# Both blocks' 32-row gate matmuls issued back to back, each in its own rows and its own bank

## The chip, the cores and the metric

The kernel runs on one core of a Trainium2 chip. The metric is the device time of one execution in microseconds (us); the time of before is the median of three runs. Five engines work side by side: PE (TensorE, matmuls), DVE (VectorE), ACT (ScalarE), POOL (GpSimd) and SP (SyncE, which here only issues DMAs). Each takes its instructions strictly in the order in which the program lists them; semaphores make one wait for another.

## The reference, cut to what matters

The program is one layer of a hybrid decoder: a gated linear attention (GLA) and a short convolution side by side, an output projection, a SwiGLU feed-forward network and norms, on 2048 positions of width 1024, in float32. The part that the change touches is the forget gate:

```python
gate_logits = (p_a @ w_gate_up[l] + b_gate[l]).astype(jnp.float32)   # p_a: rank 16, 256 gate columns
log_a = (jax.nn.log_sigmoid(gate_logits) / GATE_NORMALIZER).reshape(bsz, seq, GLA_HEADS, GLA_DK)
o = gla_chunked(q, k, v, log_a)      # cumulative sums of log_a within a chunk, exp of them on q and k
```

"The forget gate's second product" is `p_a @ w_gate_up`. Its contraction is short: 16 true rows, kept here as a high and a low part, so 32 rows.

## The kernel before, in words

Positions are cut into four blocks of 512, and two blocks make a half. The kernel goes through half 0 and half 1 in turn: the input projection `in_proj` (L596) runs twelve weight units of width 256, each by a fast matrix product of seven smaller products (`unit`, L370). A matmul of those is L366, L367 or L368 (`product_step`): the float32 operands are split into a high and a low part, so every weight quarter `wq` is made by one ACT copy (L153, high) and one DVE subtraction (L154, low), and L368 is the first matmul that needs the low part. Results are combined in `copied` (ACT, L386) and `plus` (DVE, L390).

Everything else of this stage is background work. Each is a Python generator; `tick` (L201), called after every one of the seven products, advances the first generator of the list `background` to its next `yield`. For half 0 the list holds the row statistics, `gate(0)`, then `h1_ahead` (normalised operands of half 1, made ahead); for half 1 it holds `gate(1)`, and behind it `gla_half(1)`, which `in_proj` appends when half of its units are out. The generators only give the program's order; a list scheduler then moves instructions within each engine by its own estimates, keeping every dependence.

`gate` (L547) makes one product `a` for both blocks of the half; its rows 0 to 31 belong to block j = 0, rows 32 to 63 to j = 1. Then for each block j and each half i of the 256 gate columns it issues one float32 matmul `z` (L571) of 32 rows, 128 columns and 512 positions, into a PSUM bank of its own, and calls `forget_gate` (L577). That is a chain: ACT L580 (abs) and DVE L581 read `z`; ACT L582, L583 (exp, log); DVE L584; four DVE scans L587; ACT L590 (`em`); DVE L591 (the differences `t2`); ACT L592 (`el`); DVE L593 (`dn`); and the store of `t2` to DRAM, `s_d[b][i]` (L594). After each of the four calls the generator yields.

`gla_load` (L675) reads for a chunk of 128 positions of block b, over the SP queue, q and k (`kq`), both stores `s_d[b][0]` and `s_d[b][1]` (`ee`), v (`vt`) and the output gate (`gt`). ACT L681 and L682 take exponentials of `ee`, DVE L683 and L684 multiply them into `kq`, and the PE matmuls L694 (`sc`, 64 rows each, alternating between two row groups and two banks) need both. So the first GLA chunk of a half needs both column halves i = 0 and i = 1 of that half's first block.

POOL forms sums of weight quarters (L349 to L356) and, in `h1_ahead`, differences of operands (L254 to L267).

Of the kernel before, what the change touches and what calls it, by code (L numbers as in the profile page):

```python
# [18 lines left out]
P = 128  # L19
# [32 lines left out]
def tile_hymba_block(ctx, tc, x, xt, win, wa, wgu, wout, wffn, wdown, wdown_first, small, out):  # L52
# [36 lines left out]
    wgu_sb = mixer.tile([64, 256], F32, name="wgu_sb")  # L89
# [42 lines left out]
    def col(c):  # L132
        return sml[:, c : c + 1]

    def bank(name="mm"):
        return ps.tile([P, PB], F32, name=name, tag="mm")
# [4 lines left out]
    def bt(name, shape=(P, PB)):  # L141
        return bx[0].tile(list(shape), F32, name=name, tag="b")
# [4 lines left out]
    def store(dst, src):  # L147
        return nc.sync.dma_start(dst, src)
# [398 lines left out]
    def gate(half, ops):  # L547

        a = bank("a_ps")
        names = "B11", "T1", "B21", "B22"
        for n in names:
            for k in range(4):
                q = {"B11": 3 * k + 1, "T1": 3 * k, "B21": 2 * k + 13, "B22": 2 * k + 12}[n]
                w = wa_sb[:, 32 * q : 32 * q + P]
                for e in range(2):
                    pe.matmul(
                        a[:], w, ops[n][k][:, e, :], start=(n, k, e) == ("B11", 0, 0),
                        stop=n == "B22" and k == 3 and e == 1, skip_group_check=True,  # L560
                    )
        a_sb = bt("a_sb")
        act.activation(a_sb[:], a[:], AF.Copy)
        yield
        for j in range(2):
            small = decays[2 * half + j] = [
                mtiny.tile([P, 2, PT], F32, name=n, tag=n, bufs=4) for n in ("em", "dn", "el")
            ]
            for i in range(2):
                z, r = bank("z"), slice(32 * j, 32 * j + 32)  # L570
                pe.matmul(  # L571
                    z[:], wgu_sb[r, i * P : (i + 1) * P], a_sb[r, :], start=True, stop=True
                )
                forget_gate(2 * half + j, i, z, *small)
                yield

    def forget_gate(b, i, z, em, dn, el):  # L577
        bg = col(C_BG + i)
        t1, t2 = bt("g1"), bt("g2")
        act.activation(t1[:], z[:], AF.Abs, bias=bg)  # L580
        dve.tensor_scalar(t2[:], z[:], bg, 0.0, ALU.add, ALU.min)  # L581
        act.activation(t1[:], t1[:], AF.Exp, scale=-1.0)  # L582
        act.activation(t1[:], t1[:], AF.Ln, bias=one_t)  # L583
        dve.tensor_tensor(t2[:], t2[:], t1[:], ALU.subtract)  # L584
        for t in range(PT):
            s = slice(t * P, (t + 1) * P)
            dve.tensor_tensor_scan(t1[:, s], ones[:], t2[:, s], 0.0, ALU.mult, ALU.add)  # L587
        bs = t1.rearrange("p (a b) -> p a b", b=P)
        dd = t2.rearrange("p (a b) -> p a b", b=P)
        act.activation(em[:, i, :], bs[:, :, 63], AF.Exp, scale=1.0 / 16.0)  # L590
        dve.tensor_tensor(dd, bs, bs[:, :, 63:64].to_broadcast([P, PT, P]), ALU.subtract)  # L591
        act.activation(el[:, i, :], dd[:, :, P - 1], AF.Exp, scale=1.0 / 16.0)  # L592
        dve.tensor_tensor(dn[:, i, :], em[:, i, :], el[:, i, :], ALU.mult)  # L593
        store(s_d[b][i][:], t2[:])  # L594
# [77 lines left out]
    decays = {}  # L672
# [378 lines left out]
    for i in range(4):  # L1051
# [3 lines left out]
    background.extend(  # L1055
        [
            gate_weights(), pause(9), row_stats(2), row_stats(3), gate(0, ops), unhurried(),
            h1_ahead(),
        ]
    )  # L1060
    in_proj(0, ops, first, differences)
    drain_background(lambda: len(background) < 2)
    ops = load_pairs(s_h1)
    background.append(gate(1, ops))
    in_proj(1, ops)
    drain_background(lambda: (1, PT - 1) in done)
# [119 lines left out]
```

## Time and profile before

| what | value |
|---|---|
| median of three runs | 2113.87 us (2112.77 to 2115.74) |
| the profiled execution: span from first to last instruction | 2109.1 us |
| PE busy | 2033.1 us, 96% of the span |
| DVE, ACT, POOL busy | 67%, 48%, 46% |
| `z` matmuls (L571) | 16 records for 8 calls, between 124.8 and 483.4 us |
| mean granted TensorE clock | 0.992 |

The span is the time between the first and the last instruction of one profiled execution; the time of a run also holds what lies around it, 4.8 us between this span and the median. [...] Matmul records overlap: what a matmul costs its successors is read from the distance between starts, not from its duration.

### The profile page before, as it was taken

What the parts mean: (1) busy time and instruction counts of PE and PEld (TensorE: products, weight loads), DVE (VectorE), ACT (ScalarE), POOL (GpSimd) and SP (SyncE); (2) the same over time, 40 slices, a digit from 0 to 9 for tenths busy, and PEclk for the clock granted to TensorE, in tenths of its full rate; (3) what the DMA queues carried; (4) which work ended last, traced back from release to release, by engine and by line L of the source; (5) the groups of instructions that cost most, each with busy time, mean ns of one, the idle gap of its engine ahead of it and who ended that gap; (6) DMA issues with size and microseconds to landing.
All of it is one profiled execution on the core that took longest, in us unless ns stands there. A gap on an engine that the chain in (4) does not pass through costs nothing.

```text
span 2109.1 us, 26874 instructions
## 1 busy us (share of the span) xinstructions
PE 2033.1 (96%) x9133; PEld 1648.9 (78%) x9133; DVE 1418.4 (67%) x1983; ACT 1014.1 (48%) x1997; POOL 972.4 (46%) x703
## 2 busy tenths in 40 slices
PE   5999999999999999999999999999999989999996
PEld 4778888877888878788888878787888868877775
DVE  7669786549753786788786665554766666665564
ACT  5555455656542356445545443333554554543344
POOL 3436322222102464564464348764645544436774
PEclk9999999999999999999999999999999999999998
DMA  7349485425586872656545687697454535587763
GB/s 277 126 158 318 139 329 164 148 83 164 201 284 235 325 249 100 241 198 221 217 172 220 243 327 272 235 338 296 158 207 179 206 134 190 183 344 281 269 269 110
DMA packets 189241, 464.43 MB, mean 220 GB/s; under 512 B 19824, under 2 KB 65072, under 8 KB 179504
## 3 DMA queue, kind: packets, MB, share of 16 engines
q1 hardware_dynamic: 189104, 462.72, 60.4%
q8 instruction: 72, 1.18, 0.2%
q14 instruction: 65, 0.53, 0.1%
HBM read 297.49 MB, written 165.15 MB: 219 GB/s over the span
## 4 chain that ended last, share of the span: by engine, by line
PE 70%; DVE 8%; DMA 7%; ACT 3%; issue 3%; POOL 2%; SPq 0%; DVEq 0%; ACTq 0%; POOLq 0%
PE mm L366 21%; PE mm L368 21%; PE mm L367 21%; DVE wq L154 2%; DMA op<-shT 1%; DVE so L154 1%; PE mm L794 1%; DVE h L490 1%; PE mm L795 1%; PE mm L797 1%; DVE op L154 1%; DMA sx<-y 1%; ACT wq L153 1%; PE o_ps L718 1%; DMA shT<-so 1%
## 5 line engine op out<-in xcount | busy, mean ns | idle before, releaser
L366 PE MATMUL mm<-op,wq 128*128 128x512 f32 x2499 | 981.3, 395 | 23.8 <-DVE c L390 7.8
L368 PE MATMUL mm<-op,wq 128*128 128x512 f32 x2499 | 966.1, 392 | 12.6 <-DVE wq L154 11.9
L367 PE MATMUL mm<-op,wq 128*128 128x512 f32 x2499 | 976.0, 391 | 0.0
L154 DVE TENSOR_TENSOR wq<-raw,wq 128x512 fp32r<-128x512 f32 (+2 forms) x626 | 527.3, 849 | 329.9 <-ACT wq L153 324.3
L153 ACT ACTIVATE wq<-raw 128x512 fp32r<-128x512 f32 (+2 forms) x626 | 363.6, 587 | 555.8 <-PE mm L368 402.4
L366 PEld LDWEIGHTS mm<-op,wq 128*128 128x128 f32 x2499 | 470.8, 188 | 137.6 <-ACT wq L153 12.3
L368 PEld LDWEIGHTS mm<-op,wq 128*128 128x128 f32 x2499 | 470.5, 188 | 123.5 <-DVE wq L154 24.8
L367 PEld LDWEIGHTS mm<-op,wq 128*128 128x128 f32 x2499 | 471.2, 189 | 96.7 <-issue 1.0
L351 POOL TENSOR_TENSOR raw<-s,raw 128x512 f32<-128x512 f32 (+2 forms) x97 | 127.5, 1314 | 422.2 <-DVE wq L154 402.0
L390 DVE TENSOR_TENSOR c<-mm,c 128x512 f32<-128x512 f32 x267 | 183.0, 686 | 95.7 <-PE mm L368 93.0
L349 POOL TENSOR_TENSOR s<-raw 128x512 f32<-128x512 f32 (+2 forms) x97 | 130.2, 1343 | 216.2 <-DMA raw<-in_wffn_dram 88.8
L356 POOL TENSOR_TENSOR raw<-raw 128x512 f32<-128x512 f32 (+2 forms) x97 | 126.7, 1306 | 135.3 <-DVE wq L154 128.1
L386 ACT ACTIVATE c<-mm 128x512 f32<-128x512 f32 x267 | 154.7, 585 | 38.0 <-PE mm L368 36.8
L776 POOL TENSOR_TENSOR ssx<-ssx,q 128x512 f32<-128x512 f32 x52 | 76.5, 1483 | 156.0 <-ACT q L775 155.8
L350 POOL TENSOR_TENSOR raw<-raw 128x512 f32<-128x512 f32 (+2 forms) x97 | 135.1, 1393 | 4.1
L965 POOL TENSOR_TENSOR y<-c,y 128x512 f32<-128x512 f32 x66 | 98.7, 1499 | 49.0 <-DVE c L390 46.6
L154 DVE TENSOR_TENSOR so<-t,so 128x512 fp32r<-128x512 f32 x100 | 91.2, 918 | 25.9 <-ACT so L153 25.4
L153 ACT ACTIVATE wq<-s 128x512 fp32r<-128x512 f32 (+2 forms) x97 | 56.9, 586 | 93.5 <-PE mm L368 83.3
L794 PE MATMUL mm<-op,wq 128*128 128x512 f32 x256 | 100.9, 395 | 0.0
L795 PE MATMUL mm<-op,wq 128*128 128x512 f32 x256 | 99.8, 390 | 0.0
L154 DVE TENSOR_TENSOR wq<-s,wq 128x512 fp32r<-128x512 f32 (+2 forms) x97 | 84.1, 867 | 15.6 <-ACT wq L153 15.0
L153 ACT ACTIVATE so<-t 128x512 fp32r<-128x512 f32 x100 | 62.5, 627 | 41.8 <-DMA sa_T<-so 16.1
(177 smaller groups left out, 1885.0 us busy)
## 6 DMA issues: line engine op xcount, KB each, us to landing
raw<-in_wffn_dram SPq DMA_DIRECT2D x44, 1024.0 KB, 5.7
sa_T<-so SPq DMA_DIRECT2D x88, 512.0 KB, 5.3
op<-sa_T SPq DMA_DIRECT2D x88, 512.0 KB, 9.2
sa_B<-so SPq DMA_DIRECT2D x69, 512.0 KB, 3.4
op<-sa_B SPq DMA_DIRECT2D x69, 512.0 KB, 9.0
raw<-in_win_dram SPq DMA_DIRECT2D x23, 1024.0 KB, 5.5
raw<-in_wdown_dram SPq DMA_DIRECT2D x24, 768.0 KB, 6.2
sx<-y SPq DMA_DIRECT2D x48, 256.0 KB, 3.2
```

The costliest lines, as they stand in the source:

```text
L153: last_hi[:] = [act.activation(hi, src, AF.Copy)]
L154: return dve.tensor_tensor(lo, src, hi.bitcast(F32), ALU.subtract)
L349: pool.tensor_tensor(s1, a21, a22, ALU.add)
L350: pool.tensor_tensor(a21, a11, a21, ALU.subtract)
L351: pool.tensor_tensor(a11, s1, a11, ALU.subtract)
L356: pool.tensor_tensor(a12, a12, a11, ALU.subtract)
L366: pe.matmul(o[:], wh, xh, start=first and k == 0, stop=False, skip_group_check=True)
L367: pe.matmul(o[:], wh, xl, start=False, stop=False, skip_group_check=True)
L368: return pe.matmul(o[:], wl, xh, start=False, stop=k == n - 1, skip_group_check=True)
L386: act.activation(t[:], o[:], AF.Copy)
L390: dve.tensor_tensor(t[:], o[:], t[:], ALU.add)
L794: pe.matmul(o[e, j][:], wh, m[:, 0, :], start=k == 0, stop=False)
```

## The change

The loops over column halves i and blocks j change places. Both blocks' tiles `em`, `dn`, `el` are made first; then for each i both matmuls are issued with nothing between them, into two banks, and the two calls of `forget_gate` follow, with one yield after each as before. The number of matmuls, banks, calls, yields and stores is the same. The order of the four calls was (j, i) = (0,0), (0,1), (1,0), (1,1); it becomes (0,0), (1,0), (0,1), (1,1).

```diff
         for j in range(2):
-            small = decays[2 * half + j] = [
+            decays[2 * half + j] = [
                 mtiny.tile([P, 2, PT], F32, name=n, tag=n, bufs=4) for n in ("em", "dn", "el")
             ]
-            for i in range(2):
-                z, r = bank("z"), slice(32 * j, 32 * j + 32)
+        for i in range(2):
+            z = [bank("z") for _ in range(2)]
+            for j in range(2):
+                r = slice(32 * j, 32 * j + 32)
                 pe.matmul(
-                    z[:], wgu_sb[r, i * P : (i + 1) * P], a_sb[r, :], start=True, stop=True
+                    z[j][:], wgu_sb[r, i * P : (i + 1) * P], a_sb[r, :], start=True, stop=True
                 )
-                forget_gate(2 * half + j, i, z, *small)
+            for j in range(2):
+                forget_gate(2 * half + j, i, z[j], *decays[2 * half + j])
                 yield
```

Lines below the change stand three higher in the changed kernel: `forget_gate` is L580, its differences `t2` L594, and `sc` L697.

## The prediction

> **What bounds the kernel now.** I read the page first, then the PE timeline around the `z` matmuls, then the stretches beside them, then DVE, POOL and ACT in the one stretch where something is late. What I say of the changed order is read from the list of instructions that the scheduler gives each engine in the built program.
>
> ```profile
> span 2109.1 us, 26874 instructions
> PE 2033.1 (96%) x9133; PEld 1648.9 (78%) x9133; DVE 1418.4 (67%) x1983; ACT 1014.1 (48%) x1997; POOL 972.4 (46%) x703
> PE 70%; DVE 8%; DMA 7%; ACT 3%; issue 3%; POOL 2%; SPq 0%; DVEq 0%; ACTq 0%; POOLq 0%
> ```
>
> PE is busy 96% of the span and is 70% of the chain that ended last. So a microsecond taken from PE is worth a microsecond, unless PE then waits at the next place where it is only just served. The tile view gives the removable work, the stretches say where PE has company.
>
> ```profile
> L571 PE MATMUL z<-a_sb,wgu_sb x16: 587/588/692, 124.8 to 483.4; 32*128 32x512 f32 x16
> 160.00:220.00 60.00, 59.40 (x260) 48.65 (x261) 56.90 (x66) 31.61 (x62) 38.26 (x25) 1.00 0.88 297
> 470.00:520.00 50.00, 50.00 (x239) 38.40 (x239) 47.64 (x90) 32.79 (x80) 10.86 (x8) 1.00 0.44 142
> 520.00:600.00 80.00, 80.00 (x439) 65.72 (x438) 56.91 (x109) 42.37 (x116) 9.98 (x7) 1.00 0.66 223
> ```
>
> In each stretch the busy times stand as PE, PEld, DVE, ACT, POOL. Just behind the gates of either half DVE is busy nearly all the time as well: 56.90 of 60 us, and 47.64 of 50. There PE and DVE run neck and neck, and that decides this case.
>
> **The PE time that goes.** A call alone, and two calls in series on the same rows:
>
> ```profile
> 124.44 0.39 PE L368 MATMUL mm<-op,wq 128*128 128x512 f32 x1
> 124.76 1.12 PE L571 MATMUL z<-a_sb,wgu_sb 32*128 32x512 f32 x2
> 125.81 0.50 PE L366 MATMUL mm<-op,wq 128*128 128x512 f32 x1
> 126.15 0.40 PE L367 MATMUL mm<-op,wq 128*128 128x512 f32 x1
> 126.38 0.39 PE L368 MATMUL mm<-op,wq 128*128 128x512 f32 x1
> ...
> 132.43 0.39 PE L368 MATMUL mm<-op,wq 128*128 128x512 f32 x1
> 132.75 1.98 PE L571 MATMUL z<-a_sb,wgu_sb 32*128 32x512 f32 x4
> 134.66 0.50 PE L366 MATMUL mm<-op,wq 128*128 128x512 f32 x1
> ```
>
> The normal step between two starts is 0.23 (126.15 to 126.38). Alone: 125.81 - 124.44 = 1.37, less 0.23, plus the longer step behind it (0.34 for 0.23), is 1.25. Two in series: 134.66 - 132.43 = 2.23, less 0.23, plus 0.11, is 2.11. Before has three groups in half 0 (1, 1 and 2 calls) and four single ones in half 1: 2 x 1.25 + 2.11 = 4.61 and 4 x 1.25 = 5.00. The changed order has two pairs in each half, at the places of the first and of the third call. A pair in different rows and banks costs at least one call, 1.25, and at most two in series, 2.11. Which it is near, the 64-row `sc` matmuls show, which alternate between two row groups and two banks:
>
> ```profile
> 495.10 0.37 PE L694 MATMUL sc<-kq 64*128 64x128 f32 x1
> 495.10 0.38 PE L694 MATMUL sc<-kq 64*128 64x128 f32 x2
> ```
>
> One record takes 0.37, two of different rows 0.38: they run together. I take 1.26 a pair. PE then saves 4.61 - 2.52 = 2.09 in half 0 and 5.00 - 2.52 = 2.48 in half 1, 4.57 in all; at 2.11 a pair it would be 0.39 and 0.78.
>
> [...] The 0.37 and 0.38 above speak for the larger saving, though with 128 columns; what follows needs neither.
>
> **Half 0: what is late next.** Behind the gates PE already waits, and for DVE:
>
> ```profile
> 151.46 0.50 PE L368 MATMUL mm<-op,wq 128*128 128x512 f32 x1 [2.11 <-DVE wq L154]
> 160.60 0.50 PE L366 MATMUL mm<-op,wq 128*128 128x512 f32 x1 [0.86 <-ACT c L386]
> ...
> 150.73 0.68 DVE L154 TENSOR_TENSOR wq<-s,wq 128x512 fp32r<-128x512 f32 x1
> 151.33 0.74 DVE L490 SCALAR_TENSOR_TENSOR h<-h,sml,rb_ps 128x512 f32<-128x512 f32 x1
> 151.99 1.40 DVE L154 TENSOR_TENSOR lo<-t,hi 128x512 fp32r<-128x512 f32 x1
> ```
>
> PE stood 2.11 us until DVE had split the `s` quarter. Coming 2.09 earlier only makes that wait longer, as far as DVE ends at the same time. The scheduler now lists the `h` and the `lo<-t` of this fence ahead of that split, not behind it, so the split ends up to 0.66 (151.99 - 151.33) + 1.40 = 2.1 later, while the splits after it have that work already behind them. The wait of 0.86 can disappear. DVE has the same instructions in all, and through 220 us it is at 56.90 of 60. Half 0 is therefore worth between -0.9 and +2.1; I take 0, DVE's sum being unchanged.
>
> **Half 1: the step that costs.** `gla_load` of block 2 needs both column halves of block 2. Their calls were the first and the second; now they are the first and the third, the second belonging to block 3. So the store `s_d[2][1]`, the `ee` load behind it, ACT's two exponentials, DVE's two products into `kq` and the `sc` matmuls hang on the third gate call instead of the second. PE keeps `sc` at its old place, ahead of the fourth product, and waits there in order. This is how DVE stood in before, from the scans of the third call on:
>
> ```profile
> 487.27 3.39 DVE L587 TENSOR_TENSOR_SCAN g<-ones,g 128x128 f32<-128x128 f32 x4
> 490.58 0.66 DVE L390 TENSOR_TENSOR c<-mm,c 128x512 f32<-128x512 f32 x1
> 491.16 0.74 DVE L635 SCALAR_TENSOR_TENSOR c<-u,sml,c 128x512 f32<-128x512 f32 x1
> 491.82 0.68 DVE L584 TENSOR_TENSOR g<-g,g 128x512 f32<-128x512 f32 x1
> 492.43 0.68 DVE L154 TENSOR_TENSOR wq<-raw,wq 128x512 fp32r<-128x512 f32 x1
> 493.03 0.68 DVE L591 TENSOR_TENSOR g<-g 128x512 f32<-128x512 f32 x1
> 493.63 0.42 DVE L683 TENSOR_TENSOR kq<-kq,ee 128x256 f32<-128x256 f32 x1
> 493.96 0.74 DVE L635 SCALAR_TENSOR_TENSOR c<-u,sml,c 128x512 f32<-128x512 f32 x1
> 494.63 0.42 DVE L684 SCALAR_TENSOR_TENSOR kq<-kq,ee 128x256 f32<-128x256 f32 x1
> 494.96 1.37 DVE L587 TENSOR_TENSOR_SCAN g<-ones,g 128x128 f32<-128x128 f32 x4
> ```
>
> `kq` was ready at 494.63 + 0.42 = 495.05 and `sc` began at 495.10, PE not having waited: already then there was no slack. The third call's L591 ended at 493.71. In the changed list the same instructions stand ahead of it but for one L635 (0.66 to the next start) and one split L154 (0.60). PE also reaches the third call 1.25 earlier, of which I take half, 0.6, because ACT now has two gate chains in a row (bounds 0 and 1.25). It ends at 493.71 - 1.26 - 0.6 = 491.85. Behind it:
>
> ```profile
> 493.74 0.32 SPq L148 DMA_DIRECT2D sd<-g  x1
> sd<-g SPq DMA_DIRECT2D x4, 256.0 KB, 2.1
> DMA to landing us min/median/max: 1.9/2.9/5.0
> 490.81 0.40 ACT L681 ACTIVATE ee<-ee 128x256 f32<-128x256 f32 x1
> 491.25 0.42 ACT L682 ACTIVATE ee<-ee 128x256 f32<-128x256 f32 x1
> ```
>
> The store issues 0.03 after L591 (493.74 - 493.71), lands after 2.1, the `ee` load (the third row is the tile view of `ee`, 466 to 520 us) after 2.9; the exponentials take 491.67 - 490.81 = 0.86, the last product 0.42, `sc` follows 0.05 later. 491.85 + 0.03 + 2.1 + 2.9 + 0.86 + 0.42 + 0.05 = 498.2, against 495.10 before: **+3.1**. PE would be there at 495.10 - 2.48 = 492.6, so it waits about 5.6 and its whole saving is inside that wait. Lower end: the four scans took 3.39 beside POOL's sums and 1.37 without them, 2.02 less; were that not to recur and both landings 1.9, `kq` would be there at 495.0: -0.1. Upper end: none of the 0.6, both landings 5.0: +8.7.
>
> ```profile
> 487.09 1.29 POOL L349 TENSOR_TENSOR s<-raw 128x512 f32<-128x512 f32 x1 [4.02 <-DMA raw<-in_win_dram]
> 488.46 1.29 POOL L350 TENSOR_TENSOR raw<-raw 128x512 f32<-128x512 f32 x1
> ```
>
> [...]
>
> Queued behind `sc` on PE are the transposes and the rest of the unit; the next split that PE needs, the fourth quarter's, is listed ahead of `kq` on DVE, so it is ready. From 520 to 600 PE is busy 80.00 of 80: a delay at 498 is carried to the end. What DVE has queued behind `kq` (the next `u`, then the fifth quarter's split, which PE needs later) is delayed with it, and PE is delayed as much.
>
> **Sum.** 0 for half 0 and +3.1 for half 1 on a span of 2109.1 give 2112.2; the median lies 4.8 above that span, so 2113.87 + 3.1 = **2117.0**. (0.2%, about what a measurement of this kernel can tell from no change, is 4.2 us.)
>
> **Rivals.** *The saving survives, faster.* If `kq` is not late, PE keeps 4.57: 2109.3. For it: PE is 70% of the chain. Against: the 2.11 of waiting in half 0, and 495.05 for 495.10 in half 1. Chance 0.07; half 1 alone surviving, 2111.4, another 0.10.
>
> *The wait at `sc` is dearer, clearly slower.* Two DMAs in series now stand in PE's path, on an SP queue that issues other loads between them. With landings of 5.0 each this gives +8.7, 2122.6. It counts as slower once store and load together take over 6.1 (5.0 taken, plus 4.2 - 3.1), or, together with the +2.1 of half 0, once over 4.0. Chance 0.38.
>
> *The matmuls do not overlap*: 2.11 a pair. PE then comes to `sc` at 494.3, still before 498.2, and the time is again 2117.0; contained in the others.
>
> My forecast, a wait at `sc` that costs a little more than was saved, has 0.45. With the 0.10 it makes 0.55 for within 0.2%, 0.07 faster, 0.38 slower. The range leaves out the first rival and the far end of the second: 2112.5 to 2122.
>
> **What would show it.** Right: each pair of `z` takes about 1.1 us on PE for four records; `sc` in half 1 starts near 498 with an idle time of several us ahead of it, ended by DVE `kq` (L686 or L687), DVE idle before that for ACT `ee` or the load; PE's wait near 150 us lasts 3 to 6. Wrong: no wait ahead of `sc`, or an L594 of the third call well before 490, or new waits for `wq` behind 500.

## Result, and the profile after

The changed kernel took **2122.86 us** (median of 10 runs, 2116.57 to 2126.72) beside 2113.31 us for the kernel before (10 runs, 2104.47 to 2118.0): ratio 1.0047, 95% interval 1.0033 to 1.0061, so 7 to 13 us slower. Measured again beside three of the experiments it was 2119.81 against 2113.22: 1.0033, 1.0019 to 1.0046. The forecast was 2117.0.

From the page of the changed kernel: span, the first row of part 1, and the chain of part 4.

```profile
span 2125.0 us, 26875 instructions
PE 2038.8 (96%) x9133; PEld 1654.2 (78%) x9133; DVE 1412.5 (66%) x1983; ACT 1013.9 (48%) x1997; POOL 973.8 (46%) x703
PE 74%; DVE 10%; DMA 6%; issue 3%; ACT 3%; POOL 2%; SPq 0%; DVEq 0%; ACTq 0%; POOLq 0%
```

PE's busy sum did not fall, although its two pairs in each half are faster: 2038.8 for 2033.1. A busy sum counts longer matmuls too (below, 10 fill 3.40 us at a granted clock of 0.51, where 17 fill 3.50 at 1.00); the mean granted clock is 0.987 for 0.992. The shares alone say no more, so the two traces have to be laid side by side.

**Where the time went.** PE runs 2499 matmuls of L366 in every kernel of this study. I take the start of the n-th one in each trace, counted from 0, and subtract that of before. Between the 75th (110 us in before) and the 250th (244 us) stand half 0's gates and what follows on them; between the 450th (410 us) and the 600th (546 us) those of half 1. A growing difference is time lost there.

| kernel | half 0 | half 1 | between the halves | time, ratio to before (95%) |
|---|---|---|---|---|
| changed | +6.63 | +3.83 | +0.02 | 1.0047 (1.0033 to 1.0061) |
| changed, again (e5) | +4.47 | +4.79 | +0.01 | 1.0033 (1.0019 to 1.0046) |
| e1, half 0 alone | +4.58 | -0.23 | +0.02 | 1.0009 (1.0000 to 1.0017) |
| e2, half 1 alone | +0.01 | +3.42 | 0.00 | 1.0014 (1.0005 to 1.0022) |
| e10, half 1 alone, again | -0.01 | +3.45 | +0.01 | 1.0015 (1.0004 to 1.0025) |
| e3, order without pairs | -0.21 | +4.43 | +0.02 | 1.0017 (1.0007 to 1.0028) |
| e4, pairs of one block | +4.30 | -0.27 | -0.01 | 1.0025 (1.0016 to 1.0034) |
| e6, half 0, one ACT wait mended | +2.52 | -0.22 | 0.00 | 0.9999 (0.9986 to 1.0012) |
| e7, half 0, both mended | +0.43 | -0.18 | +0.02 | 0.9999 (0.9988 to 1.0011) |
| e8, half 1: four in front | +1.11 | -1.63 | +0.03 | 0.9984 (0.9971 to 0.9996) |
| e11, the same again | +0.99 | -1.62 | +0.01 | 0.9988 (0.9978 to 0.9997) |
| e12, e7 and e8 together | +0.43 | -1.60 | +0.01 | 0.9990 (0.9978 to 1.0002) |
| e9, e2 with the wait filled | +0.08 | +1.87 | +0.03 | 0.9998 (0.9988 to 1.0008) |

The rest of a trace wanders without regard to the change: ahead of the 75th matmul the kernels stand -2.9 to +1.2, and between the 1200th and the 1350th they lose either about 0 or about 1.5; the changed kernel did both, 1.51 in its first trace and -0.12 in the second. Behind the 1350th it lost 3.41 and -0.05, and e8 and e11, which are one kernel, 5.38 and 1.51. So of the 15.9 by which the two profiled spans differ (2125.0 to 2109.1) only 10.5 are the change's, which the medians, 9.6 apart, agree with. The two profiled executions are also not alike: in every run that has both numbers on record the time is 1.7 to 2.1 above the span, so of the 4.8 between span and median of before the larger part is an execution quicker than the median, while that of the changed kernel (2126.72) was the longest of its ten.

How far a stretch wanders that nobody changed can be read from the table as well: in e2, e8, e9, e10 and e11 half 0 is that of before, instruction by instruction on every engine, and it stands between -0.01 and +1.11.

**Half 0.** The pairs do what they should. PE, timeline:

```profile
125.64 0.39 PE L368 MATMUL mm<-op,wq 128*128 128x512 f32 x1
125.96 1.13 PE L573 MATMUL z<-a_sb,wgu_sb 32*128 32x512 f32 x4
127.02 0.50 PE L366 MATMUL mm<-op,wq 128*128 128x512 f32 x1
```

Two calls of two records each, and 127.02 - 125.64 - 0.23 + 0.11 = 1.26 for both. By the 100th L366 PE is 2.13 ahead of where it was. Then it waits, for longer than before did in the same place. PE, timeline:

```profile
143.17 0.50 PE L366 MATMUL mm<-op,wq 128*128 128x512 f32 x1 [0.98 <-ACT c L386]
147.84 0.50 PE L366 MATMUL mm<-op,wq 128*128 128x512 f32 x1 [1.20 <-ACT wq L153]
149.47 0.50 PE L368 MATMUL mm<-op,wq 128*128 128x512 f32 x1 [0.90 <-DVE wq L154]
153.19 0.50 PE L368 MATMUL mm<-op,wq 128*128 128x512 f32 x1 [1.13 <-DVE wq L154]
```

These four are 4.21 together, where before had one of 2.11: the saving of 2.1 went into them, as forecast (two of the four are waits for ACT, which the forecast did not name). What was not forecast comes 50 and 70 us later, where before had no wait at all. All engines, timeline:

```profile
199.42 1.30 POOL L254 TENSOR_TENSOR t<-h 128x512 f32<-128x512 f32 x1
...
200.76 0.63 ACT L153 ACTIVATE hi<-t 128x512 fp32r<-128x512 f32 x1 [4.72 <-POOL t L254]
...
202.29 1.08 ACT L386 ACTIVATE c<-mm 128x512 f32<-128x512 f32 x2
...
202.93 0.50 PE L366 MATMUL mm<-op,wq 128*128 128x512 f32 x1 [2.19 <-ACT c L386]
...
220.02 0.90 SPq L145 DMA_DIRECT2D ee<-sd  x2
222.50 0.42 ACT L684 ACTIVATE ee<-ee 128x256 f32<-128x256 f32 x1 [5.32 <-DMA ee<-sd]
...
223.79 0.58 ACT L386 ACTIVATE c<-mm 128x512 f32<-128x512 f32 x1
...
224.42 0.50 PE L366 MATMUL mm<-op,wq 128*128 128x512 f32 x1 [2.15 <-ACT c L386]
```

ACT, 48% busy over the span, stood still for 4.72 and for 5.32 us in front of an instruction that could not start: once `hi<-t`, which needs POOL's `t`; once the exponential of the second chunk, whose `ee` load SP had only just issued. Behind it stood the copies `c<-mm` that take PE's sums out of PSUM, ready to run, and PE waited for the free bank. In the kernel before, ACT had the same instructions the other way round:

```profile
197.30 1.08 ACT L386 ACTIVATE c<-mm 128x512 f32<-128x512 f32 x2
198.76 0.63 ACT L153 ACTIVATE hi<-t 128x512 fp32r<-128x512 f32 x1 [0.38 <-POOL t L254]
...
217.55 1.07 ACT L386 ACTIVATE c<-mm 128x512 f32<-128x512 f32 x2
...
219.95 0.42 ACT L681 ACTIVATE ee<-ee 128x256 f32<-128x256 f32 x1 [0.54 <-DMA ee<-sd]
```

There the copies ran first, and the waits of `hi<-t` and of the exponential hurt nobody. The scheduler had turned both pairs round, 70 and 90 us behind the gates' last products (132.68).

**Half 1.** The forecast wait is there. All engines, timeline (with the three added lines, L594 is the L591 of before, L684 to L687 are L681 to L684, L697 is L694):

```profile
492.10 1.36 DVE L590 TENSOR_TENSOR_SCAN g<-ones,g 128x128 f32<-128x128 f32 x4
...
494.18 2.23 POOL L349 TENSOR_TENSOR s<-raw 128x512 f32<-128x512 f32 x1 [4.68 <-DVE wq L154]
...
495.77 1.18 DVE L594 TENSOR_TENSOR g<-g 128x512 f32<-128x512 f32 x1
...
496.98 0.32 SPq L148 DMA_DIRECT2D sd<-g  x1
...
498.18 0.32 SPq L145 DMA_DIRECT2D ee<-sd  x1
...
499.86 0.72 DVE L638 SCALAR_TENSOR_TENSOR c<-u,sml,c 128x512 f32<-128x512 f32 x1
...
501.26 1.72 POOL L356 TENSOR_TENSOR raw<-raw 128x512 f32<-128x512 f32 x1 [3.15 <-DVE dn L596]
501.78 1.75 DVE L638 SCALAR_TENSOR_TENSOR c<-u,sml,c 128x512 f32<-128x512 f32 x1
...
502.00 0.40 ACT L684 ACTIVATE ee<-ee 128x256 f32<-128x256 f32 x1
502.43 0.42 ACT L685 ACTIVATE ee<-ee 128x256 f32<-128x256 f32 x1
...
503.45 0.68 DVE L154 TENSOR_TENSOR wq<-raw,wq 128x512 fp32r<-128x512 f32 x1
...
504.13 0.41 DVE L686 TENSOR_TENSOR kq<-kq,ee 128x256 f32<-128x256 f32 x1
504.46 0.41 DVE L687 SCALAR_TENSOR_TENSOR kq<-kq,ee 128x256 f32<-128x256 f32 x1
...
504.93 0.58 PE L697 MATMUL sc<-kq 64*128 64x128 f32 x2 [4.52 <-DVE kq L687]
```

From the third gate's end (496.95) over store, load and exponentials to `kq` and `sc`, in the order that the prediction wrote down; PE stood 4.52 us. Then a column of the windows view that the prediction had not used, the granted clock (behind the five busy times; the first line holds the wait for ACT at 224, the second is the stretch behind it, the last one that behind the wait at `sc`):

```profile
222.00:225.80 3.80, 1.65 (x8) 1.16 (x7) 2.85 (x6) 3.27 (x7) 0.00 (x0) 1.00 0.49 137
226.00:229.40 3.40, 3.40 (x10) 2.63 (x9) 3.40 (x7) 2.03 (x6) 0.00 (x0) 0.51 0.16 19
229.50:233.00 3.50, 3.50 (x17) 2.87 (x17) 3.46 (x6) 1.45 (x3) 1.62 (x1) 1.00 0.87 353
504.90:507.20 2.30, 2.27 (x13) 2.05 (x14) 2.30 (x5) 1.25 (x4) 0.00 (x0) 0.50 0.32 83
```

PE is busy all through 226 to 229.4 and does 10 matmuls there, where the stretch behind it does 17: half speed for 3.4 us, 1.7 us lost, after a wait of 2.15. The `sc` of half 1 run at 0.50 as well. A wait can be paid twice.

### The profile page after: what moved, and what is told of

Its sections match the earlier page's. It is cut to its first block, busy times and chain, and to the rows that moved or that the text cites. A ratio compares the mean times of both kernels' runs of the same rounds, so it can differ in the third digit from the quotient of the medians.

```text
span 2125.0 us, 26875 instructions
## 1 busy us (share of the span) xinstructions
PE 2038.8 (96%) x9133; PEld 1654.2 (78%) x9133; DVE 1412.5 (66%) x1983; ACT 1013.9 (48%) x1997; POOL 973.8 (46%) x703
## 4 chain that ended last, share of the span: by engine, by line
PE 74%; DVE 10%; DMA 6%; issue 3%; ACT 3%; POOL 2%; SPq 0%; DVEq 0%; ACTq 0%; POOLq 0%
PE mm L366 21%; PE mm L368 21%; PE mm L367 20%; DVE wq L154 3%; PE mm L797 3%; PE mm L798 3%; PE mm L800 3%; DVE so L154 1%; DVE h L490 1%; DMA op<-shT 1%; DMA raw<-in_wffn_dram 1%; DVE op L154 1%; DMA raw<-in_wdown_dram 1%; ACT wq L153 1%; PE a_ps L558 1%
## 5 line engine op out<-in xcount | busy, mean ns | idle before, releaser
L366 PE MATMUL mm<-op,wq 128*128 128x512 f32 x2499 | 984.4, 396 | 29.6 <-ACT c L386 11.5
L366 PEld LDWEIGHTS mm<-op,wq 128*128 128x128 f32 x2499 | 472.4, 189 | 143.4 <-ACT c L386 15.6
L356 POOL TENSOR_TENSOR raw<-raw 128x512 f32<-128x512 f32 (+2 forms) x97 | 125.5, 1294 | 134.8 <-DVE wq L154 131.6
```

The source lines that it names most:

```text
L366: pe.matmul(o[:], wh, xh, start=first and k == 0, stop=False, skip_group_check=True)
```

## Experiments

Theory **A**: the halves cost separately. In half 0 ACT stands at instructions that the new order put ahead of the copies; in half 1 `sc` waits because block 2's second gate comes third; part of either price is the clock behind the wait. Rivals are named with each run. All variants but e5 use this helper; e1 to e4, e8, e10 and e11 differ in the loops alone:

```python
def product(i, j):
    z, r = bank("z"), slice(32 * j, 32 * j + 32)
    pe.matmul(z[:], wgu_sb[r, i * P : (i + 1) * P], a_sb[r, :], start=True, stop=True)
    return z
```

**e1 and e2: one half at a time.**

```diff
+if half == 0:                      # e2: half == 1
+    for i in range(2):
+        zs = [product(i, j) for j in range(2)]
+        for j, z in enumerate(zs):
+            forget_gate(2 * half + j, i, z, *decays[2 * half + j])
+            yield
+else:
+    for i, j in ((0, 0), (1, 0), (0, 1), (1, 1)):
+        z = product(i, j)
+        forget_gate(2 * half + j, i, z, *decays[2 * half + j])
+        yield
```

> The changed loop in half 0 alone; half 1 has the loop of before. Theory A (two separate costs: in half 0 the new order of ACT's instructions, which stops ACT behind waits at about 200 and 222 us; in half 1 the wait at sc): the half 0 part alone, from the profile after -2.1 for the overlapped pairs and +6.6 net by 227 us, so +4.5 to +7 us, 2118 to 2120, with PE waiting about 2 us for ACT's c near 203 and again near 224, and no wait ahead of sc near 500. Theory B (the half 0 difference was one profiled execution's accident, and the whole loss belongs to half 1): within 1.5 us of before, or 2 us faster. Theory C (what the profiles drift apart by behind 500 us, 4 us, belongs to the change too): more than 8 us.

> The changed loop in half 1 alone; half 0 has the loop of before. Theory A: +3 to +4 us, 2116.5 to 2117.5: sc of block 2 waits 4 to 5 us for DVE's kq, less the 2.5 that the overlapped pairs save; none of the waits for ACT near 203 and 224. Theory B: the whole +9.5. The two kernels e1 and e2 together should give the +9.5 of the full change by A.

By the traces each half has its own loss and leaves the other alone (table: +4.58 and -0.23; +0.01 and +3.42). By time e1 is 1.0009 (1.0000 to 1.0017), 1.9 us, under the expected 4.5; e2 1.0014 (1.0005 to 1.0022), 3.0 us. Theory B, all in half 1, falls by the trace of e1; theory C, a share behind 500 us, by both. Why e1's time is below its trace: the waits differ from execution to execution. Its wait at 222 was 0.28 us (2.15 in the changed kernel), while its 1.96 at 201.66 was followed by a slow clock:

```profile
202.80:206.20 3.40, 3.40 (x10) 2.63 (x9) 3.40 (x5) 1.15 (x2) 1.93 (x2) 0.50 0.67 147
```

One profile of half 0 is thus worth little to within 2 us, and I do not claim its size closer than that.

**e3 and e4: the order without pairs, the pairs without the order.**

```diff
+for i, j in ((0, 0), (0, 1), (1, 0), (1, 1)):          # e3
+    z = product(i, j)
+    forget_gate(2 * half + j, i, z, *decays[2 * half + j])
+    yield
...
+for j in range(2):                                     # e4
+    zs = [product(i, j) for i in range(2)]
+    for i, z in enumerate(zs):
+        forget_gate(2 * half + j, i, z, *decays[2 * half + j])
+        yield
```

> The call order of the change in both halves (block 0 and block 1 alternate) but each product directly ahead of its own gate, one at a time, so no pair and no overlap. By the instruction lists half 0 then stands as before; half 1 has block 2's second gate third. Theory A: half 0 costs nothing (no pair, no shift of ACT's instructions), half 1 waits at sc as in the change without the saving of 2.5 ahead of it, which the wait swallows anyway: +3 to +6 us. Theory D (pairing two gate chains is what costs in both halves, not the order of the calls): within 1 us of before and no wait at sc.

> Both products of one block issued back to back, block by block: same rows, so no overlap (2.1 us a pair), and the call order of before. ACT's order in half 0 is the one of the change. Theory A: half 0 loses as in the change and lacks 1.7 us of the saving, about +6 to +9; half 1 has block 2 ready in time, no wait at sc of more than 1 us, about -0.8 to 0: +5 to +9 in all. Theory E (the loss in half 0 comes from the changed order of the blocks, not from two gate chains side by side on ACT): -1 to +1.

e3 was 1.0017 (1.0007 to 1.0028), half 0 -0.21, half 1 +4.43; e4 1.0025 (1.0016 to 1.0034), half 0 +4.30, half 1 -0.27. The two halves fail for two different reasons, crosswise: half 1 loses by the order of the calls, whether paired or not, and half 0 by two gates side by side, whichever blocks they belong to. Theories D and E fall. The rows, `sc` of e3 first, then a pair of e4:

```profile
495.16 1.22 PE L697 MATMUL sc<-kq 64*128 64x128 f32 x8 [3.16 <-DVE kq L687]
```

```profile
123.46 0.39 PE L368 MATMUL mm<-op,wq 128*128 128x512 f32 x1
123.78 1.98 PE L572 MATMUL z<-a_sb,wgu_sb 32*128 32x512 f32 x4
125.69 0.50 PE L366 MATMUL mm<-op,wq 128*128 128x512 f32 x1
```

Same rows: 125.69 - 123.46 - 0.23 + 0.11 = 2.11 for two calls, in series; different rows: 1.26. In e4 no overlap was won, and half 0 lost about as much: how fast the products are does not decide it. That half had been expected at +6 to +9 and came at +4.30; what the pairs save in the changed kernel is lost again in the waits near 150 us, so e4, which lacks it, is no dearer.

**e5: the changed kernel again**, unedited, beside e6 to e8.

> The changed kernel once more, beside the kernels below. Theory A (the two halves cost separately and add): e1 and e2 gave +1.9 (0 to 3.6) and +3.0 (1.0 to 4.6), so +3 to +7. Theory F (the halves do more together than apart, something neither e1 nor e2 has): +8 or more again. In the trace by A: waits for ACT's c near 203 and 224 and the wait at sc near 500; the clock at 0.50 for 3.4 us (1.7 lost) behind some of them.

1.0033 (1.0019 to 1.0046), 4.0 to 9.7 us; in the trace +4.47 and +4.79, with the same waits: 2.18 at 201, 1.58 at 222, 4.51 at `sc`. e1 and e2 add to 1.0023; with their intervals that meets this run and the lower part of the first one. Theory A holds, F is not needed.

**e6 and e7: mend ACT's order, keep the pairs.** On e1. `issue_after` makes the scheduler put what stands under it behind a given instruction; `last_c` collects the copies `c<-mm`, and the 14th and 11th from the end are those that ACT should take first.

```diff
-            act.activation(t[:], o[:], AF.Copy)
+            last_c.append(act.activation(t[:], o[:], AF.Copy))
...
             o = gla_outputs(b, t, *s)
             yield
+            if half == 0 and n == 0:
+                with tc.issue_after(last_c[-14].ins):
+                    gla_scale(*nxt[:2])                # gla_load's exponentials and products
...
-            split(h[:], hi[:], lo[:])
+            with ExitStack() as stack:                 # e7 only
+                if (n, k) == ("T1", 3):
+                    stack.enter_context(tc.issue_after(last_c[-11].ins))
+                split(h[:], hi[:], lo[:])
```

> Pairs in half 0 alone (e1), and the two exponentials of the second chunk (0,1) held back behind one of the c copies of the next unit, so that ACT no longer stands for the ee load with two copies queued behind it; all else in the order of e1. Theory A: the PE wait of 0.3 to 2.2 us near 223 is gone, the one of 2 us near 202 stays: 1 to 2.5 us less than e1 by the trace, so 0 to +2.5 of before. Rival G (ACT is only where the delay shows, the copies are late since DVE or PE is late): the wait stays, at another instruction.

> As the run before it, and the hi<-t that stopped ACT 4.7 us near 200 held back behind two c copies: ACT's order between 195 and 225 us is then that of the kernel before, with the pairs of half 0 kept. Theory A: neither of the two waits, PE keeps what the pairs saved less the waits for wq and c at 142 to 167 us, which stay: -2 to +1 of before. Rival G: +2 or more, with PE waiting in the same stretch for other copies or for wq.

e6 was 0.9999 (0.9986 to 1.0012), e7 0.9999 (0.9988 to 1.0011); the times cannot tell them from before, the traces can. Waits of PE for ACT between 196 and 226 us in e6:

```profile
200.01 0.50 PE L366 MATMUL mm<-op,wq 128*128 128x512 f32 x1 [2.24 <-ACT c L386]
```

and in e7 none; its windows line over the whole stretch:

```profile
198.00:228.00 30.00, 30.00 (x133) 24.71 (x133) 29.85 (x40) 16.31 (x36) 13.70 (x9) 1.00 0.67 204
```

against that of the changed kernel:

```profile
198.00:228.00 30.00, 25.66 (x108) 20.48 (x107) 24.01 (x33) 14.62 (x32) 13.27 (x9) 0.97 0.61 191
```

Each instruction moved back took its own wait away and no other. The one near 222 us (0.28 in e1, 1.58 to 2.19 in e4, e5 and the changed kernel) is gone in e6, where the one near 200 still lasts 2.24, and that one is gone in e7. From the 180th to the 250th L366 ACT's instructions in e7 stand in the order of before, one by one. The sums close: 0.43 + 2.24 = 2.67 for e6 (2.52); 0.43 + 1.96 + 0.28 and 1.7 of clock = 4.4 for e1 (4.58); 0.43 + 2.18 + 1.58 = 4.19 for e5 (4.47); 0.43 + 2.19 + 2.15 and 1.7 of clock = 6.5 for the changed kernel (6.63). So the step from e1 to e6, +4.58 to +2.52, is for the most part the slow clock behind the wait at 201.66, which the edit of e6 does not touch; the step from e6 to e7, +2.52 to +0.43, is the wait. Rival G, the delay coming from elsewhere, falls. That ACT's order causes the two waits is shown by the traces; what they cost in time is known less well, e1 (1.0000 to 1.0017) and e7 (0.9988 to 1.0011) overlapping.

**e8 and e11: half 1 with the pairs, and block 2 ready first.** Half 0 is that of before.

```diff
+if half == 1:
+    zs = {(i, j): product(i, j) for i in range(2) for j in range(2)}
+    for i, j in ((0, 0), (1, 0), (0, 1), (1, 1)):
+        z = zs[i, j]
+        forget_gate(2 * half + j, i, z, *decays[2 * half + j])
+        yield
```

> Half 0 as before; in half 1 all four products go back to back as two overlapped pairs, and the gates then run block by block, so block 2 is ready first. By the list sc also moves some 25 PE instructions earlier. Theory A (half 1 lost because block 2's second gate came third): no wait at sc over 2 us; 2.5 saved on PE: -2.5 to +1. Rival (four gate chains side by side delay ACT's and DVE's splits, and sc waits all the same): +2 to +5, with waits for wq between 480 and 500 or at sc.

> e8 once more: by its trace half 1 saved 1.6 us against before, its ratio said 3.4 (0.8 to 6.1). Expected -1 to -3 of before, and no wait at sc.

0.9984 (0.9971 to 0.9996) and 0.9988 (0.9978 to 0.9997): 2.5 to 3.4 us faster than before, a little (e8 somewhat more than the -2.5 to +1 expected of it), and both intervals lie below 1. In the trace of e8 half 1 saves 1.63; the four calls and `sc`:

```profile
469.90 0.39 PE L368 MATMUL mm<-op,wq 128*128 128x512 f32 x1
470.22 1.99 PE L572 MATMUL z<-a_sb,wgu_sb 32*128 32x512 f32 x8
472.13 0.50 PE L366 MATMUL mm<-op,wq 128*128 128x512 f32 x1
...
490.50 0.71 PE L704 MATMUL sc<-kq 64*128 64x128 f32 x8
```

Four calls take 2.11, where the four of before took 5.00, and `sc` starts without a wait. One wait of 0.79 for a split, at 481.85, is new; 1.63 of the 2.89 is kept. This version beats both kernels, that of before by little. The times say more than the traces: in half 0, which is that of before, both traces of this kernel lost about 1 (+1.11 and +0.99), so the two halves together come to -0.5 and -0.6. What the rest of the 2.5 to 3.4 is stays open.

**e9: fill the wait.** On e2: 16 products that nobody reads, put on PE ahead of the late `sc`, and e10, e2 itself, beside it.

```diff
+        if (b, t) == (2, 0):
+            fill = ps.tile([P, P], F32, name="fill", tag="mm")
+            with tc.issue_after(last_step[0].ins):     # the last product step so far
+                for _ in range(16):
+                    pe.matmul(fill[:], ident[:], ident[:], start=True, stop=True)
```

> e2 (pairs in half 1 alone) and 16 products of the identity with itself, that nobody reads, ahead of block 2's first sc on PE; by the list 4 stand some 14 instructions ahead of sc and 12 directly ahead. The output is unchanged. Theory H (behind the wait at sc PE runs its next 1.7 to 3.4 us at a granted clock of 0.50, and that loss, not only the wait, is part of half 1's price): sc starts where it does in e2, PE's wait there shrinks from 4.5 us to under 2, no stretch at 0.50 follows, and PE is 1 to 2 us earlier than in e2 by 520 us although it does 16 matmuls more. Rival (the wait alone is the price, the clock costs nothing): as e2 or up to 2 us later.

> e2 once more, beside the kernel with the filled wait on the same chip: +3.0 (1.0 to 4.6) again; in the trace a wait of 4.5 us at sc, a stretch at clock 0.50 behind it, +3.5 between 450 and 520 us.

0.9998 (0.9988 to 1.0008) against 1.0015 (1.0004 to 1.0025): with 16 matmuls more, the kernel is faster, by 3.8 us between the medians of twelve runs each; the trace shows 1.6 of it. PE at `sc`, and the windows line of 495 to 499.2 us, of e9:

```profile
491.13 2.84 PE L704 MATMUL fill<-ident 128*128 128x128 f32 x24
494.89 0.71 PE L709 MATMUL sc<-kq 64*128 64x128 f32 x8 [0.92 <-DVE kq L694]
```

```profile
495.00:499.20 4.20, 4.20 (x27) 3.57 (x28) 4.16 (x8) 2.35 (x6) 0.00 (x0) 1.00 0.15 44
```

and of e10:

```profile
495.12 0.71 PE L704 MATMUL sc<-kq 64*128 64x128 f32 x8 [4.51 <-DVE kq L694]
```

```profile
495.00:499.20 4.20, 4.08 (x20) 3.48 (x21) 4.20 (x10) 2.45 (x6) 0.00 (x0) 0.61 0.20 47
```

`sc` starts at the same time in both (494.89 + 2.22 = 497.11 and 495.12 + 1.99 = 497.11 on before's count, each trace running that much early by the 500th L366). Only the clock differs, 1.00 for 0.61, 27 records for 20, and half 1 costs 1.87 instead of 3.45. Theory H holds: 1.6 us of half 1's price is the clock behind the wait.

**e12: the best of both halves**, half 0 of e7 and half 1 of e8.

> Half 0 of e7 (pairs, ACT's order mended) and half 1 of e8 (four products in front, gates block by block). If the halves add: 0 to +0.3 and -1.6, so -1 to -3 of before, as the kernel of e8 beside it. If the mended half 0 is worth anything by itself, 1 us or more below that.

0.9990 (0.9978 to 1.0002), +0.43 and -1.60 in the trace: the halves add, and the mended half 0 is worth nothing by itself.

## Why the prediction went wrong

- **PE saving: right.** 1.26 a pair was taken and 1.26 measured; 2.13 gained by the first 100 L366 for 2.09.
- **Half 0 = 0: this step failed.** "Half 0 is therefore worth between -0.9 and +2.1; I take 0, DVE's sum being unchanged." By the traces it was +4.5 to +6.6 (by time, e1 alone gives 1.9, 0.0 to 3.6). The reason given was sound as far as it went: with ACT's order mended (e7) half 0 is +0.43, the 2.1 saved going into longer waits for splits and one copy at 143 to 153 us, 4.21 in all in the changed kernel, inside the "3 to 6" of the prediction. But the step looked at DVE and at the stretch right behind the gates. It did not ask which instructions of ACT, half idle, had moved ahead of a copy that PE needs, and those stood 70 to 90 us behind the products: there PE waited 2.19 and 2.15 for ACT's copies (e5: 2.18 and 1.58).
- **Half 1 = +3.1: mechanism right, sizes off, and a term missing.** `sc` waited for `kq`, behind store and load on the third gate, and PE was there at 504.93 - 4.52 = 500.41, less the 7.82 by which this trace ran late by the 500th L366: 492.6, as forecast. Three sizes differ. The third gate ended 2.7 earlier than taken (496.95 - 7.82 = 489.1 for 491.85): its scans took 1.36 and not 3.39, POOL's next sum starting only at 494.18. From there to the exponentials it was 5.05 (5.0 taken). Then `kq` lost 1.3 that had not been counted, since DVE was in L638 and then in a split when the exponentials were done (502.85 to 504.13). `sc` came at 497.1, not 498.2, +2.0. The missing term is the clock: 1.4 in e2, 1.8 in the changed kernel, 2.8 in e5 (half 1's sum less the wait, plus the 2.48 saved). 2.0 and the clock make the +3.4 to +4.8 measured; +3.1 came near it by luck, two errors standing against each other. One of the prediction's signs of being wrong, an L594 of the third call well before 490, came true (487.95 to 489.1), and `sc` waited all the same.
- **DVE beside POOL: not tested at the scans.** POOL did not run beside them (1.36 in all, as the 1.37 of before without it). It did beside the L638 that stood ahead of `kq`: 1.75 us, with POOL's L356 from 501.26 to 502.98. At 499.86, with POOL idle, it was 0.72, and the 25 of this trace with POOL idle took 0.72 to 0.76. That 1.0 is most of the 1.3.
- **Carried to the end: right, as far as it can be read.** Half 0's loss stands unchanged up to half 1: between the halves the difference moves by 0.03 at most. Half 1's is not seen to come back: from the 600th to the 1200th L366 the difference moves by -1.9 to +0.6 in the six traces with that loss, and by -2.9 to -0.4 in the seven without.
- **The dearer rival** had the total, not the place: it put more than 4 us into `sc` and at most 2.1 into half 0, where half of the loss or more lay (4.5 to 6.6 beside 3.8 to 4.8). "No overlap, same time" held in half 0, where e4 tested it; in half 1, for which it was worded, no run did.

## What to carry to other kernels

When a scheduler lays out the queues, an edit can turn round two instructions far from it, and what matters is not how busy an engine is but whether one that cannot start yet now stands ahead of one that PE needs; read the lists of all engines through to the end of the changed stretch, the half idle ones first. A product that is made earlier helps only if the order in which its readers become ready stays that of the consumer: here issuing all four in front and keeping the gates block by block gained 2.5 to 3.4 us by time, alternating them lost 3. And a wait of PE should be priced with the clock behind it: here stretches at a granted 0.50 followed all five waits of 3.16 to 4.52 us and four of the fourteen of 1.96 to 2.24, with up to 1.7 us lost in each stretch, by where the wait lay.

## What the runs showed of the hardware

Two matmuls of 32 rows and 512 columns in different rows and banks took the time of one (1.26 for 1.25), four in two row groups that of two in series (2.11).

TensorE's granted clock fell to 0.50 for one or two stretches of 3.4 us after waits, 1.7 lost for each that PE worked through (10 matmuls for 17 at 226 us in the changed kernel). After the five waits of 3.16 to 4.52 us at `sc` it did so every time. Of fourteen waits of 1.96 to 2.24 us, between 148 and 225 us in all traces, four were followed by it (1.96 in e1, 2.15 in the changed kernel, two of 2.09 and 2.10) and ten not, 2.24 in e6 among them. And the two short waits near 1232 us, 0.78 and 1.51, which all fourteen traces have, were followed by it in seven: that is the 0 or 1.5 of the stretch between the 1200th and the 1350th L366.

Why one wait was punished and another not can be read from the traces. In each of the fourteen all slow stretches start on one grid of 3.413 us, to within 0.011 us; where the grid lies differs from execution to execution. I cut the traces along it between 100 and 2080 us and took the windows at full clock. Of the 59 in which PE idled 1.96 us or more in all, every one was followed by a slow window; of 49 with 1.4 to 1.95, eleven; of some 7,900 with less, none. Of the fourteen waits of about 2 us, the four that were followed had 1.89 to 2.09 us in one window, the ten others at most 1.83, the border of a window having cut them. The same wait for a split in half 0 of before (2.11, ending at 151.46) and of e2 (2.09, ending at 150.88), whose half 0 is the same: first the window of before, then that of e2 and the one behind it, windows view:

```profile
149.66:153.07 3.41, 1.61 (x7) 1.35 (x8) 3.41 (x5) 2.80 (x5) 1.30 (x1) 1.00 0.99 326
148.85:152.27 3.42, 1.40 (x6) 1.18 (x7) 3.42 (x6) 2.59 (x5) 1.45 (x2) 1.00 0.97 323
152.27:155.68 3.41, 3.41 (x10) 2.63 (x9) 3.41 (x5) 3.38 (x6) 2.80 (x2) 0.50 0.57 218
```

PE idled 3.41 - 1.61 = 1.80 in the first and 3.42 - 1.40 = 2.02 in the second; behind the first the clock stayed at 1.00. No run placed a wait against the grid, so this is read from fourteen traces and not tested.
